# Two-layer hybrid decoder: the MLP's contraction by Strassen's scheme in three of eight chunks, paired recurrence blocks, another order of the first loads

## The chip, the cores and the metric

The kernel runs on one core of one Trainium2 chip. The metric is the device time of one execution in microseconds, taken as the median over several runs. The core's engines are TensorE (PE: matmuls, with its weight loads, PEld), VectorE (DVE), ScalarE (ACT), GpSimd (POOL) and SyncE (SP, which here only issues DMAs). Each engine works through a queue of its own in order, and engines wait for one another by semaphores.

## The reference, cut to what matters

Two layers over 512 tokens of width 1024. Each layer has three token mixers side by side, one output projection, and an MLP of width 4096 with a squared relu. At the end stands one more norm.

```python
for l in range(DEPTH):                                  # DEPTH = 2
    u = rms_norm(h, attn_norm_w[l])
    proj = u @ w_in[l]                                  # columns split among the mixers
    y_hgrn = hgrn2_mixer(...)   # gated linear recurrence, 4 heads of 128, in chunks
    y_mla = mla_mixer(...)      # latent attention, 4 heads
    y_dsa = dsa_mixer(...)      # an indexer picks 128 keys per query; attention over them
    h = h + concatenate([y_hgrn, y_mla, y_dsa]) @ w_out[l]
    u = rms_norm(h, mlp_norm_w[l])
    h = h + jnp.square(jax.nn.relu(u @ w_mlp_in[l])) @ w_mlp_out[l]
return rms_norm(h, final_norm_w)
```

## The kernel before, in words

**Products.** The large products are done in split precision: each factor is the sum of a high and a low half in the fp32r type, and a product is three matmuls (high by high, high by low, low by high). A weight tile comes by DMA into a buffer `raw`; ACT or DVE copies it to `whi`, and a subtraction on DVE leaves the rest in `wlo` (128x1024 each). Products of plain f32 are used where accuracy needs them, in the recurrence for example; each such matmul shows as two records in the profile. Activations lie with channels on partitions and the 512 tokens along the free side.

**The order of the instructions.** The program first records every instruction with the buffers that it needs; a planner (`order`, `forward`, `backward`) then lists them on the engines by modelled durations (`cost`) and the length of the path behind each, and only then is the program emitted. An instruction can only be placed when its buffers are free: `CAPS` says how many buffers each tag has (5 `raw`, 5 `whi`, 5 `wlo`, 24 `un`, and in PSUM 3 banks `mm` and 5 banks `mx`), `RESERVE` keeps some back for instructions further ahead. The queues in the profile are what this planner chose. Since everything goes through the same recording helper, nearly all of the program's instructions carry one line, L491 (L1420 is a matmul emitted in `pair`), and tiles are told apart by their names: `h`, q, k and other intermediate tiles are `un` buffers, `t` temporaries, `lg`, `hw`, `hq`, `pt` special ones, `d` a copy in DRAM.

**A layer.** After the projection come the indexer, the latent attention, the recurrence (`hgrn_head`, one head at a time), the choice of keys on DVE, and the sparse attention. In `hgrn_head` the intra-chunk matrix of a head is made of four 128x128 products, and beside each a product of 64x64 for the lower left corner of the block (`Ks3`, `Qs3`, tag `hq`), written to PSUM partitions 0 to 63.

**Output projection.** In the mixers' part the 512-wide columns of h lie in DRAM (`hd`, stored by SP when they were made). The product with `w_out` goes over six k-tiles for each of eight row blocks m, then over two more. For each m, SP loads `un<-d`, and DVE adds the product to it.

**MLP.** It goes over eight chunks q of 512 hidden columns. `expand_first` makes chunk 0 by plain products; `expand(q+1)` makes each later one by Strassen's scheme in Winograd's form (seven products of 24 matmuls of 128x256 instead of eight), with sums of the halves of the input made once (`forms`) and four differences of weight tiles on DVE. `activate` applies relu and the factor of the norm per token (`rb`) in one DVE instruction, then squares. `contract(q)` multiplies the chunk by its 512 rows of `w_mlp_out`, 192 matmuls of 128x256 by four weight tiles, and DVE adds eight results of 128x512 to `self.h`:

```python
for q in range(8):
    if q < 7:
        expand(q + 1)
    contract(q)
```

In the last layer, `contract(7)` computes with tokens on partitions, after `turn` has transposed h, and `add_last` does the final norm.

Of the kernel before, what the change touches and what calls it, by code (L numbers as in the profile page):

```python
# [10 lines left out]
F32 = mybir.dt.float32  # L11
# [5 lines left out]
OP = mybir.AluOpType  # L17
# [11 lines left out]
ROUNDS = 12  # L29
# [144 lines left out]
class Op:  # L174
    __slots__ = ("eng", "run", "dur", "lat", "preds", "succs", "bufs", "idx", "level", "left", "ready",
                 "start", "end", "window", "ways", "after", "lock")
# [7 lines left out]
class Recorder:  # L184
# [38 lines left out]
    def add(self, eng, run, outs, ins, dur, lat=0.0, lock=False):  # L223
# [4 lines left out]
        op.lock = lock  # L228
# [23 lines left out]
    def order(self):  # L252

        ops = self.ops
        for op in ops:
            for p in op.preds:
                ops[p].succs.append(op.idx)
        for op in reversed(ops):
            op.level = -(op.dur + op.lat + max((self.hop(op, ops[s]) - ops[s].level for s in op.succs), default=0.0))
        best = None  # L260
        for _ in range(ROUNDS):
            try:
                result, span = self.forward()
            except RuntimeError:
                if best is None:
                    raise
# [51 lines left out]
    def forward(self):  # L318
# [25 lines left out]
        key = lambda op: (op.level, op.idx)  # L344
# [12 lines left out]
        while done < len(ops):  # L357
# [31 lines left out]
            for tag, bs in need.items():  # L389
# [4 lines left out]
                if len(s) - len(bs) < RESERVE.get(tag, 0) and max(turn[b] for b in bs) >= head[tag] + len(bs):  # L394
# [53 lines left out]
            for s in op.succs:  # L448
                o = ops[s]
                o.left -= 1  # L450
                o.ready = max(o.ready, op.end + self.hop(op, o))
# [20 lines left out]
class _Engine:  # L472
# [29 lines left out]
    def cost(self, method, named, views):  # L502
        v = dict(views)
        if method == "dma_start":
            shape = next(x for _, x in views).shape
            n = math.prod(shape) * 4
            return (60.0 if self.eng != "POOL" else 1000.0), max(100.0, n / 360.0)
        out = v.get("out") or views[0][1]
        if self.eng == "PE":
# [4 lines left out]
            if rhs.buf.r:  # L514
# [3 lines left out]
            return (130.0 if m <= 64 else 214.0), 0.0  # L518
        n = max(x.free for _, x in views)
        if self.eng == "ACT":  # L520
            d = 95.0 + n / 1.2
# [12 lines left out]
        if method == "reciprocal":  # L534
# [4 lines left out]
CAPS = {"u": 16, "un": 24, "hw": 6, "lg": 10, "pt": 3, "raw": 5, "whi": 5, "wlo": 5, "t2": 6, "mm": 3, "mx": 5, "hq": 4,  # L539
        "hS": 3, "ge": 1, "sqa": 1, "rb": 1, "c1": 20, "c4": 24, "c8": 8, "c16": 4, "bst": 1, "bmv": 1, "wi": 1}  # L540
WINDOW = 400
RESERVE = {"un": 8, "mx": 2, "t2": 2, "mm": 9, "raw": 9, "whi": 9, "wlo": 9, "sqa": 9, "rb": 9, "hw": 3, "hq": 2, "hS": 1,
           "lg": 9, "pt": 9, "u": 99}


class Build:
# [51 lines left out]
    def setup(self):  # L598
# [9 lines left out]
        nc.sync.dma_start(self.ident, a["consts"][:, 0:128])  # L608
# [8 lines left out]
        for i in range(4):  # L617
            nc.sync.dma_start(xin[i], a["x"][0, :, i * 256:(i + 1) * 256].rearrange("(t p) d -> p t d", p=128))
        self.vectors()
# [19 lines left out]

        for kt in range(KT):  # L640
# [7 lines left out]
    def vectors(self):  # L648
# [4 lines left out]
        for width, group in ((128, (("an", a["attn_norm_w"], 8),)),  # L653
# [7 lines left out]
            for key, ap, k in group:  # L661
                nc.sync.dma_start(rows[r:r + DEPTH * k, 0:width],
                                  ap.rearrange("l (k p) -> (l k) p", p=width) if k > 1 else ap)
# [9 lines left out]
        nc.gpsimd.dma_start(self.hnw, bass.AP(tensor=w.tensor, offset=w.offset, ap=[[0, 128], [128, DEPTH], [1, 128]]))  # L673
# [39 lines left out]
    def rope_tables(self):  # L713
# [3 lines left out]
        nc.gpsimd.dma_start(self.pos_i, bass.AP(tensor=pos.tensor, offset=pos.offset, ap=[[0, 128], [1, 512]]))  # L717
        self.pos_c = self.tile([128, 4], I32)
        nc.gpsimd.dma_start(self.pos_c, pos.rearrange("o (t p) -> p (o t)", p=128), allow_slow_non_contiguous=True)
# [105 lines left out]
    def finish_h(self, m, key, l, src=None):  # L825
# [3 lines left out]
        if key == "an":  # L829
            nc.sync.dma_start(self.hd[m], hm)  # L830
# [20 lines left out]
    def forms(self, m, w):  # L851

# [36 lines left out]
        nc.tt(S1, x21, x22, OP.add)  # L889
        nc.tt(S3, x11, x21, OP.subtract)  # L890
        nc.tt(S2, S1, x11, OP.subtract)
        nc.tt(S4, x12, S2, OP.subtract)
# [111 lines left out]
    def layer(self, l):  # L1004
# [166 lines left out]
        hid = {}  # L1171

        def split(t):
            hi, lo = self.tile((128, 4, 256), F32R, "whi"), self.tile((128, 4, 256), F32R, "wlo")
# [4 lines left out]
        def product(out, name, w, start, stop):  # L1179

            for m in range(2):
                o = out[:, m * 256:m * 256 + 256]
                for k in range(4):
                    xh, xl = self.X[name][k]
                    ws = [x[:, k, m * 128:m * 128 + 128] for x in w]
                    nc.tensor.matmul(o, ws[0], xh, start=start and m == 0 and k == 0, stop=False,
                                     skip_group_check=True)
                    nc.tensor.matmul(o, ws[0], xl, start=False, stop=False, skip_group_check=True)
                    nc.tensor.matmul(o, ws[1], xh, start=False, stop=stop and k == 3, skip_group_check=True)

        def activate(q, c, i, b):

            r = c if c.buf.tag == "t2" else self.t2()
            v = lambda t: t.rearrange("p (m n) -> p m n", m=2)
            tok = rb[:, i * 256:i * 256 + 256].unsqueeze(1).to_broadcast([128, 2, 256])
            nc.vector.scalar_tensor_tensor(v(r), v(c), 0.0, tok, op0=OP.max, op1=OP.mult)
            hh, hl = self.uns(2, F32R)
            nc.square(hh, r)
            nc.square(r, r)
            nc.tt(hl, r, hh.bitcast(F32), OP.subtract)  # L1200
            hid[q, i, b] = hh, hl

        def expand(q):
            W = a["w_mlp_in"][l]
            raw = {}
            for k, b in ((0, 0), (0, 1), (1, 1), (1, 0)):
                t = raw[k, b] = self.tile((128, 4, 256), F32, "raw")
                c = q * 512 + b * 256
                nc.sync.dma_start(t, W[k * 512:k * 512 + 512, c:c + 256].rearrange("(k p) n -> p k n", p=128))
            w11, w12, w22, w21 = raw[0, 0], raw[0, 1], raw[1, 1], raw[1, 0]  # L1210
            A, B, C = self.ps(), self.psm(), self.ps()
            s11 = split(w11)
            nc.tt(w11, w12, w11, OP.subtract)
            product(A, "X11", s11, True, False)
            p1 = self.t2()
            nc.copy(p1, A)
            product(B, "X12", split(w21), True, True)
            nc.vector.tensor_tensor(out=p1, in0=B, in1=p1, op=OP.add)
            activate(q, p1, 0, 0)
            nc.tt(w12, w22, w12, OP.subtract)  # L1220
            s22 = split(w22)
            nc.tt(w22, w22, w11, OP.subtract)
            product(A, "S2", split(w22), False, False)
            u = self.t2()
            nc.copy(u, A)
            product(C, "S1", split(w11), True, False)
            p5 = self.t2()
            nc.copy(p5, C)
            product(A, "S3", split(w12), False, False)
            nc.vector.tensor_tensor(out=p5, in0=A, in1=p5, op=OP.add)  # L1230
            activate(q, p5, 1, 1)
            product(C, "S4", s22, False, True)
            nc.vector.tensor_tensor(out=u, in0=C, in1=u, op=OP.add)
            activate(q, u, 0, 1)
            nc.tt(w21, w21, w22, OP.subtract)
# [467 lines left out]
```

## Time and profile before

| what | value |
|---|---|
| median of 3 runs | 1348.71 us (1348.5 to 1348.83) |
| profiled execution | 1349.72 us; span of the trace 1347.9 us |
| mean granted TensorE clock | 0.988 |
| DMA moved | 131.87 MB, mean 98 GB/s |

All views of the profile come from the one profiled execution. A row of a timeline has start, duration, engine, line, operation, tile names (out<-in), shapes and a count of neighbours that were put together; a bracket at its end gives the idle time of that engine before the row and the event that ended it. `SPq` is SP issuing DMAs, and its time in a row includes waiting. The chain that ended last is followed back from the last instruction, each step to what released it.

### The profile page before, as it was taken

Reading aid. Unit: us, or ns where it says so; the run is one execution under the profiler, and the core shown is the slowest. Engines: PE = TensorE matmul, PEld = TensorE weight load, DVE = VectorE, ACT = ScalarE, POOL = GpSimd, SP = SyncE. Lnnn points to the kernel's source line nnn. Section 1 sums busy time; section 2 is a strip of 40 time slices with the busy share of each in tenths; the row PEclk is TensorE's granted clock in tenths of the full one; section 3 lists DMA queues with packets and bytes.
Section 4 is the critical chain, followed back from the end, with each engine's and each line's share of the span. In section 5 each row is a group of like instructions: output and inputs, shape, how many; then the busy total and the mean of one; then the engine's idle time right before and its main releaser. Section 6 shows DMA issues by size and latency. Waiting matters only on the chain.

```text
span 1347.9 us, 23357 instructions
## 1 busy us (share of the span) xinstructions
PE 1310.3 (97%) x9237; PEld 1185.5 (88%) x9237; DVE 1081.2 (80%) x2208; ACT 638.7 (47%) x1152; POOL 19.6 (1%) x34
## 2 busy tenths in 40 slices
PE   7999999998999999999999999999799999999996
PEld 5788788766999999999988887987599999999996
DVE  6999999984996777866666999999399777767765
ACT  5666636373553333433344684526255333433343
POOL 1010000000000000000010000000000000000000
PEclk8999999998999999999999999999899999999998
DMA  8540222333134332332463012224423223343321
GB/s 266 156 138 11 56 60 79 109 116 120 37 121 125 95 94 79 110 125 95 133 156 89 12 48 79 71 62 134 125 63 126 86 88 106 99 126 94 94 64 63
DMA packets 137106, 131.87 MB, mean 98 GB/s; under 512 B 14069, under 2 KB 129541, under 8 KB 136997
## 3 DMA queue, kind: packets, MB, share of 16 engines
q1 hardware_dynamic: 135716, 127.62, 31.1%
q0 software_dynamic: 1280, 2.77, 0.9%
q8 instruction: 72, 1.18, 0.4%
q14 instruction: 38, 0.30, 0.1%
HBM read 121.44 MB, written 8.92 MB: 97 GB/s over the span
## 4 chain that ended last, share of the span: by engine, by line
PE 88%; DVE 7%; DMA 2%; issue 1%; ACT 1%; SPq 0%; DVEq 0%; ACTq 0%
PE mm L491 58%; PE mx L491 29%; DVE un L491 3%; PE mx L1420 1%; DVE lg L491 1%; DVE wlo L491 1%; DMA wlo<-in_x_dram 1%; DMA un<-d 1%; DVE t L491 1%; DVE c L491 1%; DMA lg<-d 0%; ACT whi L491 0%; ACT t L491 0%; SPq L491 0%; ACT un L491 0%
## 5 line engine op out<-in xcount | busy, mean ns | idle before, releaser
L491 PE MATMUL mm<-un,whi 128*128 128x256 f32 (+1 forms) x2176 | 447.3, 295 | 14.8 <-DVE un L491 14.7
L491 ACT ACTIVATE whi<-raw 128x1024 fp32r<-128x1024 f32 (+2 forms) x232 | 240.6, 1041 | 413.4 <-PE mm L491 248.5
L491 PEld LDWEIGHTS mm<-un,whi 128*128 128x128 f32 x2176 | 344.5, 189 | 29.7 <-DVE un L491 16.7
L491 DVE TENSOR_TENSOR wlo<-raw,whi 128x1024 fp32r<-128x1024 f32 (+2 forms) x250 | 297.3, 1197 | 44.5 <-ACT whi L491 39.9
L491 PE MATMUL mm<-u,whi 128*128 128x512 f32 (+1 forms) x960 | 292.1, 366 | 2.1 <-DVE c L491 1.1
L491 PE MATMUL mm<-un,wlo 128*128 128x256 f32 (+1 forms) x1088 | 275.3, 294 | 0.0
L491 PEld LDWEIGHTS mm<-u,whi 128*128 128x128 f32 x960 | 176.1, 189 | 29.4 <-issue 2.9
L491 PEld LDWEIGHTS mm<-un,wlo 128*128 128x128 f32 x1088 | 190.5, 189 | 6.1 <-issue 0.8
L491 DVE TENSOR_TENSOR un<-mm,un 128x512 f32<-128x512 f32 (+2 forms) x184 | 119.8, 662 | 91.2 <-PE mm L491 77.6
L491 PE MATMUL mx<-u,whi 128*128 128x256 f32 x736 | 189.9, 282 | 0.0
L491 PE MATMUL mm<-u,wlo 128*128 128x512 f32 (+1 forms) x480 | 159.5, 363 | 0.0
L491 PE MATMUL mm<-whi,u 128*128 128x256 f32 (+1 forms) x640 | 142.2, 305 | 0.2 <-DVE un L491 0.2
L491 PEld LDWEIGHTS mx<-u,whi 128*128 128x128 f32 x736 | 137.2, 188 | 0.0
L491 PEld LDWEIGHTS mm<-whi,u 128*128 128x128 f32 x640 | 103.1, 189 | 8.0 <-issue 4.5
L491 PE MATMUL mx<-lg,whi 128*128 128x256 f32 x448 | 107.7, 281 | 0.0
L491 PE MATMUL mx<-un,un 128*128 128x512 f32 (+4 forms) x380 | 104.5, 364 | 2.0 <-DVE un L491 1.5
L491 PE MATMUL mx<-u,wlo 128*128 128x256 f32 x368 | 102.3, 282 | 0.0
L491 PEld LDWEIGHTS mm<-u,wlo 128*128 128x128 f32 x480 | 89.0, 189 | 12.0 <-issue 0.4
L491 ACT ACTIVATE un<-t 128x512 fp32r<-128x512 f32 (+1 forms) x85 | 53.3, 628 | 66.1 <-DVE t L491 60.1
L491 PE MATMUL mm<-wlo,u 128*128 128x256 f32 (+1 forms) x320 | 83.0, 299 | 0.0
L491 PEld LDWEIGHTS mx<-un,un 128*128 128x128 f32 (+1 forms) x380 | 65.2, 188 | 18.9 <-DVE un L491 4.2
L491 PEld LDWEIGHTS mx<-lg,whi 128*128 128x128 f32 x448 | 79.6, 188 | 0.0
(200 smaller groups left out, 1960.5 us busy)
## 6 DMA issues: line engine op xcount, KB each, us to landing
raw<-in_w_mlp_in_dram SPq DMA_DIRECT2D x64, 512.0 KB, 3.8
raw<-in_w_mlp_out_dram SPq DMA_DIRECT2D x64, 512.0 KB, 4.1
raw<-in_w_in_dram SPq DMA_DIRECT2D x42, 512.0 KB, 3.7
d<-un SPq DMA_DIRECT2D x20, 256.0 KB, 2.5
raw<-in_w_in_dram SPq DMA_DIRECT2D x18, 256.0 KB, 3.1
raw<-in_w_out_dram SPq DMA_DIRECT2D x16, 256.0 KB, 2.7
raw<-in_w_out_dram SPq DMA_DIRECT2D x8, 512.0 KB, 3.4
un<-d SPq DMA_DIRECT2D x16, 256.0 KB, 4.6
```

Source lines behind the costliest of these rows:

```text
L491: real(*[res(v) for v in args], **{k: res(v) for k, v in kw.items()})
L1420: self.real.tensor.matmul(outs[i].get(), vals[i].get(), rhs[i].get(), start=k == 0, stop=k == NT - 1)
```

## The change

1. `contract(q)` for q = 1, 3, 5 is done by the same seven products as `expand`, by a shared function `seven`; the other chunks keep the old code (`contract_plain`). The four weight sums of a chunk are made on DVE in the `raw` tiles, which gives seven tiles to split instead of four. The sums of the hidden blocks (`sums`) take four DVE instructions of 512, and S1 to S4 are split into halves. The results leave PSUM by 28 additions or subtractions of 256 columns in place of 8 of 512.
2. The token factor is left out of `activate` in all chunks but the last. The MLP's output is summed in new tiles `self.o`, without h; ahead of the last chunk, `residual` multiplies the sums by the factor's square and adds h, which is read again from DRAM (so h is now stored there ahead of the MLP too: 8 stores and 8 loads more per layer).
3. In `hgrn_head` two products of 128x128 over pairs of blocks take the place of the four of 64x64, and two copies pick the four 64x64 corners out of them.
4. The planner makes 24 rounds with random displacements of the levels in the later ones, tries several sets of reserves, and has some other modelled costs; there are 26 `un` and 4 `wlo` buffers now.
5. At the start SP first loads the identity, the first input tile, `attn_norm` and the second input tile; the other two input tiles come later. Three small DMAs move from POOL's queue to SP's. Three matmuls on input tiles are added, whose results nobody reads.

In all, PE has 8806 instructions instead of 8963, DVE 2285 instead of 2114, ACT 1161 instead of 1042, SP 377 instead of 342, POOL 35 instead of 38.

```diff
-ROUNDS = 12
+ROUNDS = 24
+SEED = 1
+SPREAD = 50.0
...
+            for op, x in zip(ops, rng.normal(0.0, SPREAD, len(ops)) if SEED and i > 6 else ()):
+                op.level += x
...
-                op.end = dma_free + 900.0
+                op.end = dma_free + 2200.0
...
-            return (130.0 if m <= 64 else 214.0), 0.0
+            return (300.0 if n < 128 else 130.0 if m <= 64 else 214.0), 0.0
...
-        if key == "an":
-            nc.sync.dma_start(self.hd[m], hm)
+        nc.sync.dma_start(self.hd[m], hm)
...
+    def sums(self, S1, S2, S3, S4, x11, x12, x21, x22):
+        nc = self.nc
+        nc.tt(S1, x22, x21, OP.subtract)
+        nc.tt(S3, x11, x21, OP.subtract)
+        nc.vector.scalar_tensor_tensor(S2, S1, -1.0, x11, op0=OP.mult, op1=OP.subtract)
+        nc.vector.scalar_tensor_tensor(S4, S2, -1.0, x12, op0=OP.mult, op1=OP.subtract)
...
+        def seven(t, ap, X, A, B, C, done):
+            product(A, X["X11"], split(t[0, 0]), True, False)
+            done("P1", A)
+            nc.tt(t[0, 0], t[0, 0], t[0, 1], OP.add)
+            nc.tt(t[0, 1], t[0, 1], t[1, 1], OP.add)
+            product(C, X["S1"], split(t[0, 0]), True, False)
+            done("P5", C)
+            nc.tt(t[0, 0], t[0, 0], t[1, 1], OP.add)
+            product(A, X["S2"], split(t[0, 0]), False, False)
+            done("U2", A)
+            nc.tt(t[0, 0], t[0, 0], t[1, 0], OP.add)
+            product(B, X["X12"], split(t[1, 0]), True, True)
+            done("P2", B)
+            product(A, X["S3"], split(t[0, 1]), False, False)
+            done("U3", A)
+            product(C, X["S4"], split(t[1, 1]), False, True)
+            done("P53", C)
+            product(A, X["X22"], split(t[0, 0]), False, True)
+            done("U4", A)
...
         def contract(q):
...
+            A, B, C = [self.ps(), self.ps()], [self.psm(), self.psm()], [self.ps(), self.ps()]
+            def done(name, banks):
+                for i, c in {"P1": [(0, 0)], "P2": [(0, 0)], "P5": [(1, 1)], "P53": [(0, 1)], "U2": [(0, 1)],
+                             "U3": [(1, 1)], "U4": [(1, 0)]}[name]:
+                    for j in range(2):
+                        for m in range(2):
+                            x = banks[j][:, m * 256:m * 256 + 256]
+                            o = self.o[c * 4 + j * 2 + m][:, i * 256:i * 256 + 256]
+                            nc.vector.tensor_tensor(out=o, in0=o, in1=x, op=OP.subtract if c else OP.add)
+            seven(t, ap, X, A, B, C, done)
+        def residual():
+            sq = self.un()
+            nc.vector.tensor_tensor(out=sq, in0=rb, in1=rb, op=OP.mult)
+            for m in range(KT):
+                h = self.un()
+                nc.sync.dma_start(h, self.hd[m])
+                o = self.o[m]
+                nc.vector.tensor_tensor(out=o, in0=o, in1=sq, op=OP.mult)
+                nc.vector.tensor_tensor(out=o, in0=o, in1=h, op=OP.add)
+            self.h = self.o
...
-        for q in range(8):
-            if q < 7:
-                expand(q + 1)
-            contract(q)
+        for q in range(Q - 1):
+            expand(q + 1)
+            (contract if q in SEVEN else contract_plain)(q)
+        residual()
+        contract_plain(Q - 1)
...
-            nc.tensor.matmul(pa[0:64, t * 128 + 64:t * 128 + 128], Ks3[:, t, :], Qs3[:, t, :], start=True, stop=True)
...
+        for e in range(2):
+            ts = slice(e * 128, e * 128 + 128)
+            nc.tensor.matmul(pz[:, ts], Ks[:, ts], Qs[:, ts], start=True, stop=True)
...
+        z4 = pz.rearrange("p (t e j) -> p t e j", e=2, j=64)
+        for e in range(2):
+            nc.copy(at[0:64, e:4:2, 64:128], z4[e * 64:e * 64 + 64, 0:2, e, :])
```

**SP, between the output projection and the MLP of the first layer.** `d_64` to `d_71` are the eight row blocks of h in DRAM, `raw` the weight tiles (the number behind a name tells one buffer's use from another). Before:

```order
L491 DMA raw_3496<-in_w_mlp_in_dram 128x4x256
L491 DMA un_3528<-d_64 128x512
L491 DMA un_3532<-d_65 128x512
L491 DMA raw_3578<-in_w_mlp_in_dram 128x4x256
L491 DMA raw_3626<-in_w_mlp_in_dram 128x4x256
L491 DMA raw_3674<-in_w_mlp_in_dram 128x4x256
L491 DMA un_3678<-d_66 128x512
L491 DMA un_3680<-d_67 128x512
L491 DMA un_3682<-d_68 128x512
```

The same place after (`d_64` and `d_65` are loaded some ten rows further up):

```order
L499 DMA un_3502<-d_66 128x512
L499 DMA un_3514<-d_67 128x512
L499 DMA un_3527<-d_69 128x512
L499 DMA un_3531<-d_68 128x512
L499 DMA raw_3622<-in_w_mlp_in_dram 128x4x256
...
L499 DMA raw_3738<-in_w_mlp_in_dram 128x4x256
L499 DMA un_3745<-d_70 128x512
L499 DMA un_3747<-d_71 128x512
L499 DMA d_64<-un_3294 128x512
L499 DMA raw_3795<-in_w_mlp_in_dram 128x4x256
```

Before, six of the eight blocks are loaded behind the MLP's first four weight tiles; now six are loaded ahead of them and two behind five of them, and stores of the new h follow between weight tiles. In the second layer the order is of the same kind.

**DVE, in the contraction of a chunk.** `wlo<-raw,whi` is the low half of a weight tile, `un<-mm,un` an addition of a result to h. Before, in a chunk of the second layer:

```order
L491 TENSOR_TENSOR wlo_12239<-raw_12025,whi_12225 128x1024
L491 TENSOR_TENSOR un_10962<-mm_12052,un_10962 128x512
L491 TENSOR_TENSOR un_10790<-mm_12186,un_10790 128x512
L491 TENSOR_TENSOR un_10792<-mm_12189,un_10792 128x512
L491 TENSOR_TENSOR wlo_12283<-raw_12084,whi_12271 128x1024
```

After, in chunk 1 of the first layer, where `mx_4939`, `mx_4942` and others are the banks A, B and C of the seven products, and `raw<-raw,raw` is a weight sum:

```order
L499 TENSOR_TENSOR wlo_4982<-raw_4649,whi_4960 128x1024
L499 TENSOR_TENSOR un_4681<-un_4681,mx_4939 128x256
L499 TENSOR_TENSOR raw_4649<-raw_4649,raw_4849 128x1024
L499 TENSOR_TENSOR un_4550<-un_4550,mx_4942 128x256
L499 TENSOR_TENSOR un_4559<-un_4559,mx_4942 128x256
L499 TENSOR_TENSOR wlo_5027<-raw_4649,whi_5012 128x1024
L499 TENSOR_TENSOR t_1146_4732<-mm_4827,t_1146_4732 128x512
L499 TENSOR_TENSOR raw_4649<-raw_4649,raw_4817 128x1024
```

Additions of 256 columns, weight sums and low halves alternate there, and each addition reads a bank into which PE writes again later.

**PE, in the recurrence of the first layer.** `hq` are the operands of the 64x64 products; rows with `mm` are the projection's matmuls between which the planner puts the recurrence. Before:

```order
L491 MATMUL mx_2240<-hw_1405,un_1320 128x128
L491 MATMUL mm_2219<-u_202,wlo_2057 128x512
L491 MATMUL mx_2240<-hq_2183,hq_1587 64x64
L491 MATMUL mm_2219<-u_219,whi_1808 128x512
L491 MATMUL mx_2240<-hw_1405,un_1320 128x128
```

After:

```order
L499 MATMUL mx_2282<-k_93,hw_2210 128x128
L499 MATMUL mm_2254<-u_224,wlo_2090 128x512
L499 MATMUL mx_2300<-hq_2264,hq_2215 128x128
L499 MATMUL mm_2254<-u_250,whi_2060 128x512
L499 MATMUL mm_2157<-u_338,whi_1905 128x512
L499 MATMUL mm_2254<-u_271,whi_2060 128x512
L499 MATMUL mx_2300<-hq_2264,hq_2215 128x128
```

A head's four small products in the bank of the large ones have become two of full width in a bank of their own.

More of the change, by code (lines that the diff above doesn't have):

```diff
@@ L260, in order @@
         best = None
[L261 to L266, printed above, removed]
+        rng = np.random.default_rng(SEED)
+        for i in range(ROUNDS):
+            for reserve in RESERVES[i % 3:]:
+                try:
+                    result, span = self.forward(reserve)
+                    break
+                except RuntimeError:
+                    continue
+            else:
                 break
@@ L393, in forward @@
                     break
-                if len(s) - len(bs) < RESERVE.get(tag, 0) and max(turn[b] for b in bs) >= head[tag] + len(bs):
+                if len(s) - len(bs) < reserve.get(tag, 0) and max(turn[b] for b in bs) >= head[tag] + len(bs):
                     short = tag
@@ L607, in setup, with load @@
         self.ident = c[:, O_ID:O_ID + 128]
-        nc.sync.dma_start(self.ident, a["consts"][:, 0:128])
+        early = iter(range(10, 0, -1))
+        def load(out, x, **kw):
+            nc.sync.dma_start(out, x, **kw)
+            nc.ops[-1].early = 1e9 * next(early)
+        load(self.ident, a["consts"][:, 0:128])
         self.tri = c[:, O_TRI:O_TRI + 512]
@@ L638, in setup @@
             self.at.append(t)
+        for i in (2, 3):
+            x_in(i, nc.sync.dma_start)
+        for i, n in ((0, 1), (1, 2)):
+            for _ in range(n):
+                nc.tensor.matmul(self.ps(), xin[i][:, 0, 0:128], xin[i][:, 0:2, :], start=True, stop=True)
         for kt in range(KT):
@@ L888, in forms @@
         S1, S2, S3, S4 = (self.S[n][:, k % 2, :] for n in ("S1", "S2", "S3", "S4"))
[L889 to L892, printed above, removed]
+        self.sums(S1, S2, S3, S4, x11, x12, x21, x22)
         if k % 2:
@@ L1177, in split @@
             return hi, lo
[L1179 to L1189, printed above, removed]
@@ L1203, in expand @@
-        def expand(q):
[L1204 to L1210, printed above, removed]
-            A, B, C = self.ps(), self.psm(), self.ps()
[L1212 to L1235, printed above, removed]
-            product(A, "X22", split(w21), False, True)
-            activate(q, A, 1, 0)
@@ new lines, in weights, with product @@
+        def weights(W, rows, cols):
+            r, c = W.shape[0] // 2, W.shape[1] // 2
+            ap = {(k, b): W[k * r:k * r + r, b * c:b * c + c].rearrange("(k p) n -> p k n", p=128)
+                  for k in range(2) for b in range(2)}
+            t = {}
+            for i in ((0, 0), (1, 0), (0, 1), (1, 1)):
+                t[i] = self.tile((128, r // 128, c), F32, "raw")
+                nc.sync.dma_start(t[i], ap[i])
+            return t, ap
+        def product(outs, x, w, start, stop):
+            for j, out in enumerate(outs):
+                for m in range(2):
+                    o = out[:, m * 256:m * 256 + 256]
+                    cs = slice(j * 256 + m * 128, j * 256 + m * 128 + 128)
+                    for k, (xh, xl) in enumerate(x):
+                        ws = [t[:, k, cs] for t in w]
+                        nc.tensor.matmul(o, ws[0], xh, start=start and m == 0 and k == 0, stop=False,
+                                         skip_group_check=True)
+                        nc.tensor.matmul(o, ws[0], xl, start=False, stop=False, skip_group_check=True)
+                        nc.tensor.matmul(o, ws[1], xh, start=False, stop=stop and k == len(x) - 1, skip_group_check=True)
@@ new lines, in expand @@
+        def expand(q):
+            t, ap = weights(a["w_mlp_in"][l][:, q * 512:q * 512 + 512], 512, 256)
+            A, B, C = self.ps(), self.psm(), self.ps()
+            p = {}
+            def done(name, banks):
+                x = banks[0]
+                if name in ("P1", "P5", "U2"):
+                    p[name] = self.t2()
+                    nc.copy(p[name], x)
+                    return
+                if name == "U4":
+                    activate(q, x, 1, 0)
+                    return
+                y, *block = {"P2": ("P1", 0, 0), "U3": ("P5", 1, 1), "P53": ("U2", 0, 1)}[name]
+                nc.vector.tensor_tensor(out=p[y], in0=x, in1=p[y], op=OP.add)
+                activate(q, p[y], *block)
+            seven(t, ap, self.X, [A], [B], [C], done)
@@ L1569, in hgrn_head @@
         pk = self.ps()
+        pz = self.ps()
         for t in range(NT):
```

110 lines of the change are left out of this document (75 added, 35 removed).

## The prediction

> **What bounds the kernel now.** I read the page's busy times and chain first, then the busy times by stretch of the run, then the chain and the timelines of the places that the change touches. The page:
>
> ```profile
> PE 1310.3 (97%) x9237; PEld 1185.5 (88%) x9237; DVE 1081.2 (80%) x2208; ACT 638.7 (47%) x1152; POOL 19.6 (1%) x34
> PE 88%; DVE 7%; DMA 2%; issue 1%; ACT 1%; SPq 0%; DVEq 0%; ACTq 0%
> ```
>
> TensorE (PE) is busy for 97% of the span and carries 88% of the chain that ended last. A matmul that goes away is worth its full slot, as long as PE stays fed. VectorE (DVE) at 80% is the next engine, so I ask stage by stage how near it is to the bound (stretch; then busy time and count of PE, PEld, DVE, ACT, POOL; clock; DMA share; GB/s):
>
> ```profile
> 30.00:90.00 60.00, 57.41 (x296) 47.06 (x295) 58.10 (x157) 33.91 (x57) 7.70 (x11) 1.00 0.60 169
> 90.00:270.00 180.00, 180.00 (x1073) 149.75 (x1072) 171.72 (x495) 97.80 (x228) 0.00 (x0) 1.00 0.22 65
> 400.00:680.00 280.00, 279.85 (x2385) 278.64 (x2384) 204.60 (x247) 100.96 (x122) 1.83 (x3) 1.00 0.35 106
> 915.00:945.00 30.00, 27.93 (x146) 20.03 (x144) 29.57 (x94) 22.51 (x57) 0.00 (x0) 1.00 0.34 103
> 1025.00:1325.00 300.00, 299.91 (x2568) 299.46 (x2567) 218.17 (x265) 124.58 (x162) 1.09 (x2) 1.00 0.31 96
> ```
>
> Two things are to be seen. In the MLP stretches (400:680 and 1025:1325) PE never idles and DVE is at 73%: matmuls bound, with a quarter of DVE free. In the mixers' stretches DVE is at 95 to 99%. With 95.4% PE lost nothing (90:270); with 98.6% it lost 2.07 of 30 us, 6.9% (915:945). So a crowded DVE may cost nothing or some 7%, and these two rows are my bounds for every term in which the change loads DVE.
>
> **The change part by part, first the contraction.** Three of eight chunks take 168 matmuls of 128x256 where they took 192: 24 x 3 x 2 layers = 144 fewer. Their slot, from the chain of the MLP:
>
> ```profile
> 509.95 6.62 PE mm L491 x58
> ```
>
> 6.62 / 58 = 0.114 us, so 144 x 0.114 = **16.4 us less**. What DVE pays is read from its start-to-start distances in a stretch without gaps (the durations printed are longer, since neighbours overlap):
>
> ```profile
> 993.17 0.42 DVE L491 TENSOR_TENSOR un<-un,un 128x256 f32<-128x256 f32 x1
> 993.51 0.68 DVE L491 TENSOR_TENSOR un<-mm,un 128x512 f32<-128x512 f32 x1
> 994.11 1.22 DVE L491 TENSOR_TENSOR wlo<-raw,whi 128x1024 fp32r<-128x1024 f32 x1
> 995.24 0.42 DVE L491 TENSOR_TENSOR un<-un,un 128x256 fp32r<-128x256 f32 x1
> ```
>
> That is 0.34 us for 256 columns, 0.60 for 512, 1.13 for 1024. The program issues expand(q+1) and contract(q) as a pair. A pair with the new contraction needs of DVE 22 operations of 1024 (14 lower halves of weights, 8 weight sums), 28 adds of 256, 14 operations of 512 and, by my guess, two relus: 24.9 + 9.5 + 8.4 + 1.2 = 44.0 us. PE needs 336 x 0.114 = 38.3 us for it. A pair with a plain contraction needs 15 x 1.13 + 15 x 0.60 = 26.0 us of DVE against 360 x 0.114 = 41.0 of PE. So the new pair is over the bound by itself (115%), the plain one far under it (63%), and they alternate: 70.0 of 79.3 us, 88%. Work can move across a pair's border only as far as buffers go (five raw, five high and four low weight tiles, five mx banks). A further new wait stands inside the new contraction: bank A is added out after its second and third products while one more product, 24 x 0.114 = 2.7 us, runs in another bank, and the four adds of 0.34 between take 1.4 of that. An add that stands behind one lower half (1.13) just fits; behind two it holds PE. Bounds: 0, as in 90:270, and 6.9% lost over the six new pairs, 6 x 38.3 / 0.931 - 6 x 38.3 = 17.0 us. Neither row is nearer (88% on the mean, 115% inside), so I take the middle, **8 us more**.
>
> **Token factor.** 56 multiplications leave the relu; 32 operations of 512 (16 per layer, 9.6 us) come in `residual()` between the additions of chunk 6 and those of chunk 7, with eight loads of h. Their cover is chunk 7's own 192 matmuls (21.9 us), which need no sum but do need their banks emptied; in the last layer the transposes of h wait for the residual too. Bounds 0 and 9.6 us; I take **1 us more**, since the DVE of that moment has just come out of a plain pair. The 16 additional stores and 16 loads of 256 KB (8.4 MB) go into DMA engines that are busy for 0.31 to 0.35 in the rows above: nothing. On SP, stores of the MLP's h stand ahead of the sixth mlp_in tile and wait for its sums; the first chunk's five tiles are ahead of them and cover that. ACT, at 36 to 42% in these rows, takes relus and copies at nothing.
>
> **Recurrence.** The 64x64 products stand between full matmuls:
>
> ```profile
> 899.98 0.38 PE L491 MATMUL mx<-hw,un 128*128 128x128 f32 x2
> 900.12 0.48 PE L491 MATMUL mm<-u,whi 128*128 128x512 f32 x1
> 900.53 0.33 PE L491 MATMUL mx<-hq,hq 128*64 128x64 f32 x2
> 900.79 0.50 PE L491 MATMUL mm<-u,whi 128*128 128x512 f32 x1
> 901.12 0.38 PE L491 MATMUL mx<-hw,un 128*128 128x128 f32 x2
> ...
> 902.26 0.85 PE L491 MATMUL mm<-u,whi 128*128 128x512 f32 x3
> 902.95 0.28 PE L491 MATMUL mx<-un,hw 128*128 128x128 f32 x1
> ...
> 905.01 0.38 PE L491 MATMUL mx<-un,k 128*128 128x128 f32 x2
> 905.23 0.39 PE L491 MATMUL mx<-un,hw 128*128 128x128 f32 x2
> 140.00:270.00 130.00, 130.00 (x792) 107.16 (x791) 123.92 (x367) 64.17 (x158) 0.00 (x0) 1.00 0.26 74
> 835.00:905.00 70.00, 70.00 (x454) 60.11 (x455) 66.50 (x187) 31.89 (x79) 0.00 (x0) 1.00 0.20 57
> ```
>
> One matmul in f32 is two records (x2). The 128x128 kind takes 905.23 - 905.01 = 0.22 us, a 512 one (902.95 - 902.26) / 3 = 0.23. From 899.98 to 901.12 lie 1.14 us with one 128x128 kind, two 512 ones and one 64x64 kind, which so takes 1.14 - 0.22 - 0.46 = 0.46 us, twice the larger one. The change has 32 of them (four per head, eight heads) replaced by 16 of 128x128: 14.7 - 3.5 = 11.2 us of PE. [...] But this work lies where DVE has 190.4 of 200 us (last two rows): PE cannot gain more than 9.6 us there. Bounds 0 and 11.2; I take **8 us less**. The two small copies per head go mostly to ACT, half idle there.
>
> **The order of the loads before the MLP.** SP is one queue, and h is reloaded through it (first SP, then who waits; bracket: idle time before and its releaser):
>
> ```profile
> 296.33 14.12 SPq L491 DMA_DIRECT2D raw<-in_w_mlp_in_dram  x3
> 310.54 3.09 SPq L491 DMA_DIRECT2D un<-d  x6
> 315.02 1.34 DVE L491 TENSOR_TENSOR un<-mm,un 128x512 f32<-128x512 f32 x2 [3.61 <-DMA un<-d]
> 315.77 1.22 PE L491 MATMUL mm<-un,whi 128*128 128x512 f32 x2 [5.75 <-DVE un L491]
> 944.82 14.18 SPq L491 DMA_DIRECT2D raw<-in_w_mlp_in_dram  x4
> 959.12 4.00 SPq L491 DMA_DIRECT2D un<-d  x6
> 964.75 2.09 DVE L491 TENSOR_TENSOR un<-mm,un 128x512 f32<-128x512 f32 x3 [5.03 <-DMA un<-d]
> 965.50 1.22 PE L491 MATMUL mm<-un,whi 128*128 128x512 f32 x2 [6.74 <-DVE un L491]
> 316.00:320.00 4.00, 4.00 (x11) 3.14 (x12) 1.05 (x2) 0.84 (x1) 0.00 (x0) 0.59 0.44 165
> 966.00:972.00 6.00, 6.00 (x17) 4.63 (x16) 2.01 (x3) 1.06 (x1) 0.00 (x0) 0.57 0.13 49
> 15.00:19.00 4.00, 4.00 (x15) 2.98 (x14) 3.29 (x6) 3.25 (x6) 0.00 (x0) 0.52 1.08 364
> ```
>
> Three and four weight tiles wait on SP for 14 us for a free buffer; six loads of h stand behind them, the sums of w_out's product wait for h, its banks stay full, and PE stands for 5.75 and 6.74 us. After each the granted clock is 0.59 and 0.57 for 4 and 6 us, another 1.6 and 2.6. Together 16.7 us. In the new order six of the eight loads stand ahead of those tiles, two still behind them. Bounds 0 and 16.7; six eighths are 12.5, and the two late ones can hold the last sums, so I take **11 us less**. If it goes, the next thing late is the MLP's first weight tile.
>
> **Input first.** The second input tile moves ahead of the first weight tile, the fourth falls back behind one weight tile more:
>
> ```profile
> 12.87 0.45 PE L491 MATMUL mx<-k,wlo 128*128 128x128 f32 x1 [5.92 <-DMA wlo<-in_x_dram]
> ```
>
> PE waits 5.92 us here, and then runs at 0.52 for 4 us (last row of the fence before, 1.9 us lost): at most 7.8 less if all of it went. A 512 KB tile at that row's 364 GB/s is 1.4 us, the price if the fourth one is what is late. Nearer to the second, as the DMA share of 1.08 shows no spare rate: **2 us less**. The planner's other new numbers change the order everywhere; PE idles so little outside the places named that I take 0 for it, between 5 less and 5 more.
>
> **Sum.** -16.4 + 8 + 1 - 8 - 11 - 2 = -28.4. The profiled execution took 1349.7 us (span 1347.9 and 1.8 around it), so 1321.3; it lies 1.0 above the median of the runs, which gives **1320 us**.
>
> **Rivals.** (a) DVE becomes the bound of the whole MLP. For it: 88% on the mean, 115% in three pairs of each layer, and 28 adds that each hold a bank. Against it: 95.4% without a loss in 90:270. At 915:945's loss, over both layers' 2 x 2832 x 0.114 = 646 us of matmuls, 646 x 0.069 / 0.931 = 48 us instead of 8: 1360 us, slower. It decides from a loss of 8 + 28.4 = 36 us on, 5.6% of PE's time there. (b) The gap before the MLP stays, because the last two loads of h hold it as six did: 11 more, 1331. For it: they stand behind five weight tiles, more than before. Against it: the six sums ahead of them empty banks. (c) The pairing saves nothing, because the slot goes by columns, or because DVE sets that stage: 8 more, 1328. (d) All of it pays: -16.4 - 11.2 - 16.7 - 5 = -49.3, 1299. For it only that PE idles so little elsewhere.
>
> **How the numbers follow.** The forecast's own case, 1310 to 1326, has a chance of 0.48; (b) 0.14; (c) 0.12; (d) 0.11; (a) 0.10; a DVE loss between, which ends within 0.2% (2.7 us, about what a measurement of this kernel can tell from no change) of the old time, 0.05. The range 1302 to 1340 holds the first three and a part of (d), and takes in 17 instead of 8 for the crowding together with (b) or with (c). Faster: 0.48 + 0.14 + 0.12 + 0.11 = 0.85; same 0.05; slower 0.10.
>
> **What would show it.** PE's records fall by 144 and by some 30 more; in the MLP's stretches DVE rises to about 88% and PE idles for under 3% of the time, with waits on DVE's un adds (more than 5%, and (a) holds). The 5.75 and 6.74 us before w_out's matmuls shrink to about 2, with no stretch at 0.6 behind them. No 64-column matmul is left, and the full ones around the new pair stand 0.22 apart. The first input wait is shorter by 2. Wrong would make it: new gaps of PE in the mixers' stretches, where the new order has 3% of DVE to spare at most, or a wait for `residual()` longer than 10 us.

## The result, and the profile after

The changed kernel takes 1310.4 us (1310.1 to 1311.4) against 1348.8 for the one before: a ratio of 0.9716, with a 95% interval of 0.9699 to 0.9733. It is 38.4 us faster, 10 more than forecast and inside the range. The page after (busy times, then the chain):

```profile
PE 1290.3 (99%) x9067; PEld 1171.8 (90%) x9067; DVE 1144.1 (87%) x2379; ACT 691.5 (53%) x1271; POOL 17.8 (1%) x31
PE 86%; DVE 11%; issue 1%; ACT 1%; DMA 1%; SPq 0%; DVEq 0%; ACTq 0%
```

The span fell by 39.1 us: TensorE's busy time by 20.0, and its idle time by the other 19.1. The busy time by stretch, for the places of the prediction (start; mixers; the way into the first MLP; the first MLP; the way into the second; the second):

```profile
15.00:19.00 4.00, 4.00 (x21) 3.02 (x20) 4.00 (x8) 3.90 (x7) 0.00 (x0) 1.00 0.74 210
90.00:270.00 180.00, 179.71 (x1074) 150.83 (x1074) 177.98 (x522) 100.69 (x242) 0.00 (x0) 1.00 0.23 67
300.00:316.00 16.00, 16.00 (x72) 12.54 (x71) 9.35 (x15) 4.51 (x8) 0.00 (x0) 1.00 0.47 150
400.00:680.00 280.00, 276.60 (x2262) 272.23 (x2261) 242.66 (x338) 128.87 (x176) 5.58 (x8) 1.00 0.39 121
935.00:960.00 25.00, 25.00 (x118) 20.11 (x117) 18.67 (x32) 14.28 (x26) 0.00 (x0) 1.00 0.55 174
1000.00:1300.00 300.00, 299.27 (x2519) 298.85 (x2519) 256.09 (x376) 141.98 (x217) 1.10 (x2) 1.00 0.32 101
```

The gaps ahead of both MLPs are gone altogether (300:316 and 935:960: PE full, clock 1.00). In the mixers DVE is at 98.9% and PE still loses only 0.29 of 180 us. In the MLPs DVE rose to 87 and 85%, and PE idles for 1.2 and 0.2%. So far this is the forecast, or better.

The surprise stands in the MLP itself. I split both traces by the MLP's matmul records (from the hundredth of a layer to its thirtieth from the end in the first layer, to its last in the second), which gives stages of the span in us:

| kernel | mixers 1 | MLP 1 | mixers 2 | MLP 2 | tail | span |
|---|---|---|---|---|---|---|
| before | 353.0 | 327.5 | 323.2 | 333.5 | 10.7 | 1347.9 |
| after | 337.5 | 326.5 | 307.1 | 329.7 | 8.0 | 1308.8 |

The mixers gave 31.6 us, the MLPs only 4.8, although they have 144 matmuls less. Start to start, the MLP's 128x256 matmuls take 117.5 ns on the mean before and 120.1 after; without the intervals over 140 ns, which hold a wait, it is 116.7 and 118.6. A clean stretch of the last contraction of the first layer shows it, before and then after:

```profile
651.00:672.00 21.00, 21.00 (x184) 20.79 (x183) 12.28 (x16) 5.96 (x9) 0.00 (x0) 1.00 0.52 150
624.00:660.00 36.00, 36.00 (x303) 35.76 (x302) 30.22 (x45) 13.03 (x19) 1.81 (x3) 1.00 0.59 174
```

21.00 / 184 = 114.1 ns, 36.00 / 303 = 118.8 ns, of the same shape, in the same code, without a gap and at a clock of 1.00. Was this the load on DVE, which the prediction feared, or something else?

### The profile page after: what moved, and what is told of

Same layout as the page of the kernel before. It is cut to its first block, busy times and chain, and to the rows that moved or that the text cites. A ratio compares the mean times of both kernels' runs of the same rounds, so it can differ in the third digit from the quotient of the medians.

```text
span 1308.8 us, 23399 instructions
## 1 busy us (share of the span) xinstructions
PE 1290.3 (99%) x9067; PEld 1171.8 (90%) x9067; DVE 1144.1 (87%) x2379; ACT 691.5 (53%) x1271; POOL 17.8 (1%) x31
## 4 chain that ended last, share of the span: by engine, by line
PE 86%; DVE 11%; issue 1%; ACT 1%; DMA 1%; SPq 0%; DVEq 0%; ACTq 0%
PE mm L499 50%; PE mx L499 34%; DVE un L499 5%; DVE wlo L499 2%; PE mx L1525 2%; DVE t L499 1%; DVE c L499 1%; DVE raw L499 1%; DMA wlo<-in_x_dram 1%; DVE lg L499 1%; ACT t L499 0%; ACT un L499 0%; DVE k L499 0%; DVE whi L499 0%; SPq L499 0%
## 5 line engine op out<-in xcount | busy, mean ns | idle before, releaser
L499 ACT ACTIVATE whi<-raw 128x1024 fp32r<-128x1024 f32 (+1 forms) x232 | 238.5, 1039 | 285.0 <-PE mm L499 134.3
L499 PE MATMUL mm<-un,whi 128*128 128x256 f32 (+1 forms) x1504 | 316.5, 303 | 1.2 <-ACT whi L499 0.7
L499 PEld LDWEIGHTS mm<-un,whi 128*128 128x128 f32 x1504 | 238.4, 188 | 17.7 <-issue 6.5
L499 PE MATMUL mm<-un,wlo 128*128 128x256 f32 (+1 forms) x752 | 202.0, 303 | 0.0
L499 PEld LDWEIGHTS mm<-un,wlo 128*128 128x128 f32 x752 | 133.2, 188 | 7.4 <-issue 2.0
L499 PE MATMUL mx<-un,whi 128*128 128x256 f32 x640 | 123.1, 282 | 0.3 <-DVE t L499 0.3
L499 PE MATMUL mx<-un,un 128*128 128x256 f32 (+3 forms) x380 | 102.4, 365 | 1.8 <-DVE un L499 1.3
L499 ACT ACTIVATE t<-mx 128x512 f32<-128x512 f32 (+3 forms) x137 | 62.6, 486 | 71.2 <-PE mx L499 68.7
L499 PEld LDWEIGHTS mx<-un,whi 128*128 128x128 f32 x640 | 98.8, 189 | 0.9 <-DVE t L499 0.5
L499 DVE TENSOR_TENSOR raw<-raw,raw 128x1024 f32<-128x1024 f32 x80 | 97.1, 1216 | 0.1
```

The costliest lines, as they stand in the source:

```text
L499: real(*[res(v) for v in args], **{k: res(v) for k, v in kw.items()})
```

## The experiments

**Addresses or load.** SBUF addresses, read from the two programs, gave the lead: before, `un`, `whi` and `wlo` started at multiples of 64 bytes; after, `un`, `u`, `whi`, `wlo` and `raw` were 32 bytes off such a multiple, because tiles are laid out in the order of their first use. The six runs of this part change addresses alone; the order of every instruction stays.

```diff
+        for tag, shape in (("wlo", (128, 4, 256)), ("raw", (128, 4, 256)), ("whi", (128, 4, 256)), ("un", (128, 512)), ("u", (128, 512)), ...):
+            self.sb.tile(list(shape), F32, tag=tag, bufs=CAPS.get(tag, 1), name=f"first_{tag.strip('+')}")
         self.nc.emit()
```

> The changed kernel with the same order of instructions; only the SBUF addresses differ: the large buffer groups (wlo, raw, whi, un, u, hw, lg, pt, hq) are laid out first, each tile at a multiple of 128 bytes, where in the changed kernel wlo, raw, un, u and whi start 32 bytes off a multiple of 64. Observation behind it: a 128x256 matmul of the MLP takes 118.6 ns there, and in the kernel before the contraction's took 113.4 in clean stretches, where un, whi and wlo lay at multiples of 64, while those on u (32 off) took 118. Theory A (address): the slot falls to 113.4 to 114.5, 5400 MLP matmuls x 4.5 ns = 24 us less, so about 1286 us. Theory B (load: the slot is longer because DVE and ACT do more beside it): no change, 1310 within 2.

It took 1316.4 us (1316.0 to 1317.1): slower by 6, where theory A said faster by 24 and B no change. The same layout for the kernel before:

> The kernel before, same order, same address layout as in the run before this one. Its contraction already had aligned operands (113.4 ns in clean stretches, 115.6 on the mean), its expansion did not. Theory A: the expansion's matmuls fall from 118 to 114 ns, 2700 x 4 ns = 11 us, and the contraction's between them a little, so 1348.7 - 11 to 16 = about 1335 us. Theory B: 1348.7 within 2.

It took 1363.0 us, 14.2 more than before (ratio 1.0105, 1.0089 to 1.0121). So addresses alone move both kernels, and the sign of A was wrong. The stretches of the same matmuls (aligned before, aligned after):

```profile
659.00:680.00 21.00, 21.00 (x175) 20.88 (x174) 11.36 (x16) 5.72 (x8) 0.00 (x0) 1.00 0.52 148
627.00:663.00 36.00, 36.00 (x300) 35.81 (x299) 29.92 (x43) 12.66 (x19) 1.62 (x3) 1.00 0.57 174
```

Both now take 120.0 ns, at DVE loads of 54 and 83%: load does not set the slot here. What was left was not alignment but the distance between the two operands of a matmul: the stationary one, which PEld's record loads as 128x128 (here weights), and the moving one, 128x256 in PE's record (here activations). In the aligned layout both lie at equal places modulo 512 bytes.

```diff
-        for tag, shape in (("wlo", ...), ("raw", ...), ("whi", ...), ("un", ...), ...
+        for tag, shape in (("wlo", ...), ("raw", ...), ("whi", ...), ("space", (128, 8)), ("bmv", (128, 8)), ("un", ...), ...
```

> The changed kernel, same order, in the layout of the aligned run with one difference: a spacer of 64 bytes stands between the weight tiles (wlo, raw, whi: multiples of 128) and the activations (un, u, hw, lg, pt: 64 beyond a multiple of 128). In the aligned layout every 128x256 matmul took 120.0 ns, in the kernel before those on un (64 beyond) with whi and wlo (multiples of 128) took 113.4. Theory A2 (the slot hangs on where the moving operand lies relative to the stationary one within 128 bytes): 113.4 to 114 ns for all MLP matmuls, 5472 x 6.3 = 34 us less than the aligned run's 1316.4, so 1282 us. Rival C (something else in the old layout, such as the distance of the groups or which tags stand side by side): 1310 to 1317.

1304.7 us (1304.4 to 1304.9), 11.7 less than aligned, about a third of what A2 said. And with the spacer ahead of all groups:

> As the run before this one, but the spacer stands ahead of all groups, so that weights and activations alike lie 64 beyond a multiple of 128. Theory A2 (relative position): 120 ns, 1316 within 2, like the aligned run. Rival A3 (it is the moving operand's own address that counts): 113.4 ns and 1282.

1315.7 us, as A2 said: for this shift of 64 bytes the relative place counted, not the place itself. The two stretches (64 bytes between, 36.00 / 305 = 118.0 ns; then none, 36.00 / 300 = 120.0):

```profile
621.00:657.00 36.00, 36.00 (x305) 35.74 (x304) 30.47 (x44) 13.24 (x19) 1.65 (x3) 1.00 0.57 175
627.00:663.00 36.00, 36.00 (x300) 35.82 (x299) 29.91 (x44) 13.19 (x18) 2.22 (x3) 1.00 0.56 165
```

I then joined the addresses with the records of all traces so far. Moving minus stationary modulo 512 was 0 for the 120.0 ns, 64 for a mean of 117.3, and 448 and 320 for the kernel before's contraction. So the next layout has the activations first and the weights 64 further:

> The changed kernel, same order, with the activations (un, u, hw, lg, pt) laid out first at multiples of 512 from their start and the weight tiles 64 bytes further within 512: moving minus stationary is 448 modulo 512. In the traces so far the 128x256 slot by that difference is 120.0 ns at 0, 117 to 118 at 64, and 113.4 in clean stretches at 320 and 448 (the kernel before's contraction). Theory A4 (the difference modulo 512 sets the slot, 448 is a fast one): 113.4 to 114.5 ns, 5472 x 3.5 = 19 us less than the 1304.7 of the run with the difference at 64, so about 1286. Rival A5 (only the difference modulo 128 counts, and what was fast before was fast for another reason): 117 ns and 1305 again.

1302.1 us (1301.3 to 1302.7; ratio to before 0.9654, 0.9638 to 0.9670): the fastest kernel of this study, 8.3 us under the changed one, but not the 1286 of theory A4. Its start-to-start times are of two kinds, 113 to 114 ns for 50% of the matmuls and 117 to 119 for 49%, in runs of dozens. One stretch of each kind (113.3 and 117.8 ns start to start; the counts include matmuls that reach over the borders):

```profile
344.50:361.50 17.00, 17.00 (x153) 17.00 (x152) 16.06 (x26) 12.72 (x19) 0.00 (x0) 1.00 0.29 88
497.50:516.50 19.00, 19.00 (x163) 19.00 (x163) 19.00 (x29) 8.91 (x14) 0.00 (x0) 1.00 0.36 112
```

Some 70% of the changes of kind have an interval over 140 ns, in which PE stood for a moment, within a few matmuls. At 64 the fast kind has 11%, at 0 none. What picks the kind is open. A part of the shorter slot also goes into waits: in the MLP stages the intervals over 140 ns exceed the slot by 15 us in sum here, by 11 at 64 and by 7 in the aligned layout. The kernel before in that layout:

> The kernel before, same order, in the layout of the run before this one. Theory A4: its expansion's slot falls from 118 and the contraction's mean from 115.6 to 113.4 to 114.5, 5616 x 3 = 17 us less than 1348.7, so about 1332; the change is then worth 46 us between equal layouts, as between the aligned ones (1363.0 and 1316.4). Rival A5: 117 ns everywhere, 1348 within 3.

1344.3 us, 4.5 less than before: far nearer A5's 1348 than A4's 1332, with the same two kinds. Between equal layouts the change is worth 46.6 us (aligned) or 42.2 (this one); 38.4 was measured because the old kernel's addresses happened to be better than the new one's.

**The scheme of the contraction.** From here all kernels but the one with another seed have the aligned layout, where the slot is a constant 120 ns and no luck of addresses enters.

```diff
-        SEVEN = (1, 3, 5)
+        SEVEN = ()
```

> The changed kernel in the aligned layout with all eight chunks contracted plainly (no Strassen there; token factor, residual, recurrence, planner and start as changed; the planner orders anew). Against the aligned changed kernel it has 144 more matmuls. Theory A (address): with the slot equal in both, the scheme is worth 144 x 0.114 = 16.4 us less its real crowding, so this one is 10 to 16 us slower than the aligned changed kernel, about 1299. Theory B (the scheme's DVE load lengthens the slot): its slot is about 114 and the changed one's 118.6, so it is within 4 us of the changed kernel, about 1312 whatever the layout.

1337.0 us against 1316.4: the scheme is worth 20.6 us, more than theory A's 10 to 16 and than its own 144 x 0.120 = 17.3. Theory B is out again: the slot is 120.0 with and without it. At this slot the crowding of DVE that I priced at 8 us cost nothing: the intervals over 140 ns in the MLP stages exceed the slot by 7.4 us in sum with the scheme and by 7.9 without. At a shorter slot the scheme was not taken back alone.

**The recurrence.** Pairing taken back:

```diff
+            nc.tensor.matmul(pa[0:64, t * 128 + 64:t * 128 + 128], Ks3[:, t, :], Qs3[:, t, :], start=True, stop=True)
...
-        for e in range(2):
-            ts = slice(e * 128, e * 128 + 128)
-            nc.tensor.matmul(pz[:, ts], Ks[:, ts], Qs[:, ts], start=True, stop=True)
...   (and the two corner copies)
```

> The changed kernel in the aligned layout with the recurrence's old four 64x64 products per head (no pairing, no corner copies); the planner orders anew. The prediction's step: 16 fewer matmuls and 0.46 against 0.22 us, 11.2 us on PE, 8 of them real, so about 1324 against the aligned 1316.4. Rival (records of hq alone: 64 of them took 8.3 us before, 32 now 2.8): 5 to 6 us slower, 1322. Rival (the slot goes by columns): within 1 us.

1330.1 us, 13.7 more, beyond every expectation. In the stages, the second layer's mixers are 3.9 us longer (310.6 against 306.7), the first layer's 9.5. Most of the excess of the first layer stands in one place far ahead of the recurrence, whose small products begin at 186 us; there the new order makes PE wait (small-products kernel, waits of PE; then the stretch 20:90 of it and of the aligned kernel):

```profile
46.37 0.97 PE L499 MATMUL mx<-un,un 128*128 128x512 f32 x3 [1.64 <-ACT un L499]
50.77 0.39 PE L499 MATMUL mx<-un,un 128*128 128x256 f32 x1 [1.16 <-ACT un L499]
53.52 2.99 PE L499 MATMUL mx<-un,un 128*128 128x256 f32 x9 [2.36 <-DVE un L499]
20.00:90.00 70.00, 63.54 (x310) 52.45 (x309) 62.76 (x169) 37.64 (x67) 2.76 (x5) 0.95 0.57 173
20.00:90.00 70.00, 67.33 (x347) 54.56 (x346) 68.53 (x180) 40.38 (x75) 7.59 (x11) 1.00 0.64 194
```

Over the first layer's whole stage PE idles for 3.5 us more (9.6 against 6.2), and the clock of 0.95 in the stretch 20:90 costs another 3.5. Of the 9.5 us that leaves 2.5. So the pairing itself is worth some 6.4 us in the two layers, and the rest is what this order happened to lose.

**The start.** Old order of the first loads:

```diff
-            nc.ops[-1].early = 1e9 * next(early)
...
-        x_in(0)
-        self.vectors(load)
-        x_in(1)
+        for i in range(4):
+            x_in(i)
+        self.vectors(load)
...   (and the three matmuls on the input, the three small DMAs)
```

> The changed kernel in the aligned layout with the old order of the first loads (all four input tiles asked for first in the program, no priority, no warm-up matmuls on the input, the three small DMAs back on POOL). The prediction's step said 2 us. By the traces the first wait fell from 5.92 to 1.66 us and the clock stays at 1.00 over 15 to 19 where it was 0.52 before: 4.3 + 1.9 = 6 us, so 1322 against 1316.4. Rival (the start is caught up later, since loads set the pace there): within 2 us of 1316.4.

1324.8 us, 8.4 more; 5.0 of the span stand in the first mixers' stage. The waits of PE there (old-start kernel), then the one of the changed kernel:

```profile
12.54 0.63 PE L499 MATMUL mx<-k,wlo 128*128 128x128 f32 x4 [2.66 <-DMA wlo<-in_x_dram]
48.90 0.97 PE L499 MATMUL mx<-un,un 128*128 128x512 f32 x3 [1.64 <-DVE un L499]
53.58 6.65 PE L499 MATMUL mx<-un,un 128*128 128x256 f32 x22 [3.25 <-DVE un L499]
10.09 1.06 PE L499 MATMUL mx<-k,wlo 128*128 128x128 f32 x8 [1.66 <-DMA wlo<-in_x_dram]
```

The input waits sum to 0.89 + 2.66 there against 1.66, some 2 us; the waits at 48.9 and 53.6 come with this order too. How much of the 5.0 is the input's own and how much the new order's stays open. Expectation and rival both missed.

**The planner's numbers**, taken back in the changed kernel and put alone into the one before:

```diff
-ROUNDS = 24
-SEED = 1
+ROUNDS = 12
+SEED = 0
...
-                op.end = dma_free + 2200.0
+                op.end = dma_free + 900.0
...   (and RESERVES, CAPS, the other modelled durations)
```

> The changed kernel in the aligned layout with the planner's old numbers (12 rounds without displacement, one set of reserves, old modelled durations, 24 un and 5 wlo buffers); contraction, token factor, recurrence and input order stay changed. Theory P (the planner's numbers removed the gap before the MLP and other idle time of PE): the gaps come back, 15 to 25 us slower than the aligned changed kernel. Rival Q (the gaps went because the instructions themselves changed, the numbers do little): within 5 us of the aligned changed kernel.

1337.8 us, 21.4 more: theory P's size, but not its mechanism, since of the gaps only two of 1.66 us came back. The loss stands nearly everywhere: 6.6 and 4.9 us in the two layers' mixers, 7.1 in the second MLP and 2.1 in the tail. The other direction:

> The kernel before in the aligned layout with nothing of the change but the planner's new numbers (rounds with displacements, sets of reserves, modelled durations, 26 un and 4 wlo buffers). The aligned kernel before took 1363.0 us with PE idle for 5.76 and 6.85 us ahead of w_out's last matmuls. Theory P (these numbers alone close that gap and tighten the rest): the gaps fall under 1 us and the clock stays at 1.00 behind them, 16.7 us, and with the further order about 1342, as undoing them in the changed kernel cost 21.4. Rival Q (the gap went because the changed parts made the planner order anew; with the old numbers in the changed kernel only two waits of 1.66 us came back there): 1355 to 1363.

1346.5 us against the aligned 1363.0: 16.5 less, between the two. The gaps are gone there, as P said, and so is the slow clock behind them, 1.00 in the last row here (two rows of waits in the changed kernel with old numbers; the way into the first MLP with the new numbers alone):

```profile
308.38 0.73 PE L499 MATMUL mm<-un,whi 128*128 128x512 f32 x2 [1.66 <-DVE un L499]
949.91 0.73 PE L499 MATMUL mm<-un,whi 128*128 128x512 f32 x2 [1.66 <-DVE un L499]
295.00:330.00 35.00, 35.00 (x167) 25.99 (x165) 21.70 (x45) 17.00 (x34) 0.00 (x0) 1.00 0.40 128
```

Either the new numbers or the new instructions suffice to break the old order of the loads; the gap was a weakness of one order, not of the kernel.

**How much a mere order is worth.** Seed 2 in place of 1:

> The changed kernel in the same layout again, with the planner's seed 2 in place of 1: the same instructions in another order of the same planner. It tells how much a new order alone is worth, and so how far single differences between kernels that were ordered anew can be trusted. If the order is well determined by the model, within 2 us of the run two before this one; if it is a matter of luck, 3 to 8 us above it.

1302.9 us (1302.2 to 1304.7) against 1302.1, both with the activations laid out first. So for these instructions a second seed finds an equally good order; no third was tried. Where instructions or modelled durations were changed, the new orders did lose some us, as the waits above show. The undone parts sum to 20.6 + 13.7 + 8.4 + 21.4 = 64 us, though the whole is 46.6: each kernel was ordered anew, and a single difference holds that loss too.

The stages of the aligned kernels, in which the parts can be told apart (the profiled execution of the first row took 3.1 us more than that kernel's median):

| kernel, aligned | mixers 1 | MLP 1 | mixers 2 | MLP 2 | tail | span |
|---|---|---|---|---|---|---|
| before | 354.6 | 335.1 | 322.7 | 341.3 | 10.6 | 1364.3 |
| before, new planner's numbers | 348.3 | 335.0 | 311.1 | 341.3 | 7.7 | 1343.4 |
| after, plain contraction | 337.5 | 338.0 | 308.2 | 343.9 | 7.5 | 1335.1 |
| after | 337.3 | 329.9 | 306.7 | 333.0 | 8.0 | 1314.9 |

## Why the prediction was right

The time lay 9.6 us under the forecast, the sign and the largest reasons were right, and several terms were off in both directions. That it came so near is in part luck: in an equal layout the gain would have been 42.2 to 46.6 us, 1302 to 1306.5, at the lower end of the range, and addresses that the sum did not know took 4 to 8 us back. Step by step:

- **144 matmuls, -16.4.** Right: 17.3 by the aligned slot, and the MLP stages of the last two rows differ by 8.1 + 10.9 = 19.0.
- **Crowding of DVE in the MLP, +8.** Mis-sized: at the aligned slot of 120 ns it is nothing. The view of pairs (115 and 63%) was right on the load (87 and 85% measured, 88 forecast), but buffers carry work across a pair's border, and PE idled for 3.4 and 0.7 us in 580. The row 90:270 was the nearer bound; the middle was not called for.
- **Token factor, +1.** Not isolated. In the place that I named, around the residual and the last chunk, PE of the changed kernel waits only once, for 0.48 us at 661.77 in the first layer, and not at all in the second. But with plain contraction the MLP stages are 2.9 and 2.6 us longer than before's, 5.5 in all, where the new planner's numbers alone leave them unchanged. These 5.5 us are spread over the stages, no single wait carries them, and no run takes the token factor back alone, so which part of the change they belong to stays open.
- **Recurrence, -8.** Nearly right, a little too large: 3.9 us in the second layer, 2.5 in the first once its waits and its slow clock are taken out. Rival (c) falls by this. Its first reason, a slot that goes by the columns, fits the two widths of the fp32r matmuls before (114.1 ns at 256 in the clean stretch, a median of 232 at 512), but not these products in plain f32: start to start, the 64 records of the small ones (64 columns, before) take 129 ns each on the mean, the 32 of the large ones (128 columns, after) 86, and a 512-column matmul right in front takes 410 ns (median) before a small product and 316 before a large one. Why the small ones are slow is not shown.
- **The loads before the MLP, -11.** Mis-sized: all of it went, 16.7; the new planner's numbers alone shorten the mixers' stages by 6.3 + 11.6 us. The two late loads of h hold nobody, as the row 300:316 shows; SP issues them at 308.69, but the sums ahead of them keep banks free:

```profile
299.87 8.73 SPq L499 DMA_DIRECT2D raw<-in_w_mlp_in_dram  x3
308.69 0.93 SPq L499 DMA_DIRECT2D un<-d  x2
```

- **Input first, -2.** Mis-sized: the first wait fell from 5.92 to 1.66 us and the clock at 15:19 from 0.52 to 1.00, 6.2 us by the traces; undoing it cost 5.0 in that stage, some of it by waits of the new order.
- **The rest of the order, 0.** The tail after the last matmul shrank by 2.7 us, and the planner's numbers alone do that (10.6 to 7.7). I had left it at nothing because the change doesn't touch `add_last`. Of the 33.3 us that the aligned mixers' stages gave, the loads, the pairing and the start account for 27 to 29; the rest isn't traced to a step.
- **What was not in the sum: addresses.** Layout gave the old kernel 14.2 us against the aligned one and the new kernel 6.0, so 8.2 us of the gain were lost by that comparison, and 3.8 (42.2 less 38.4) by the layout with the activations first; no row of the trace before could show it. The slot of 114.1 ns, on which the first term rests, came from a lucky pair of addresses; over all of the old kernel's MLP matmuls it was 116.7.

Rival (a), DVE as the bound, is out: the loss in the MLPs is 4 us, not 36. Rival (b) is out. Rival (d), all of it pays, came nearest in its terms; the addresses and the 5.5 us in the MLPs kept the time from its 1299.

## What to carry to other kernels

Where a planner or a pool lays out memory in order of first use, an edit moves addresses, and here addresses alone moved the kernel before by 14.2 us (1.05%) and the changed one by 6.0 one way and 8.3 the other: compare two kernels in one fixed layout before crediting an edit. A load on DVE that was over the bound in every second pair (115% by the forecast's count) cost nothing here at the aligned slot, with waits of 7.4 us in the MLP stages against 7.9 without the scheme; the row of a full stretch that lost nothing (90:270) was the one to price by. The gap that hung on the order of one queue was worth all of its idle time and the slow clock behind it, 16.7 us, and it went with either kind of new order.

## What the runs showed of the hardware that I had not expected

All of this is measured in the traces of these runs, start to start, and joined with the SBUF addresses that the programs give their tiles. The slot of the MLP's 128x256 fp32r matmuls, each with its own weight load, went with where the moving operand lies relative to the stationary one, counted modulo 512 bytes: 120.0 ns at 0 (eight kernels, at two absolute places 64 bytes apart), 117.3 on the mean at 64 (the spacer of 64 bytes), 115.5 at 448 (activations first). At 448 it took one of two values, 113.4 or 117.8, which held for dozens of matmuls. This is shown for layouts in which nearly all MLP matmuls have one distance. In the changed kernel's own layout five distances (0, 128, 160, 288, 384) alternate, and the slot is 118.3 to 119.0 ns at each of them, at 0 too; so something else counts as well. A matmul's neighbours, or places 32 bytes off a multiple of 64, are my guess, and no run separates the two. The 128x512 slot went the other way (median 227 ns at 0, 230 at 64, 233 at 448, 232 in the two original layouts), so one cost per column does not fit both widths. Other distances were not tried alone, and which event picks the value stays open.
